# The low halves of the split weights: formed by an accumulating DMA in place of a VectorE subtraction

## The chip, the core and the metric

The kernel runs as one program on one core of a Trainium2 chip. The metric is the device time of one execution in microseconds (us). The engines named below are TensorE (PE in the profile, with its weight loads as PEld), VectorE (DVE), ScalarE (ACT), GpSimd (POOL) and SyncE (SP), beside the 16 DMA engines of the core that move data between HBM and the on-chip memory (SBUF).

## The reference

Two transformer-like blocks work on 512 tokens of 2048 features; the first one adds 16 meta tokens ahead of them. Cut to what matters here:

```python
# first block
proj = einsum('bld,dc->blc', rmsnorm(h, pre_norm_g), w_in)      # q, k, v, gates of two mixers
ya = gqa_axial_mixer(qa, ka, va, ...) * silu(ga)                # softmax attention, 8 heads
yb = diff_attn_mixer(qb, kb, vb, ...) * silu(gb)                # difference of two softmaxes, 8 heads
h = h + rmsnorm(einsum('blc,cd->bld', concat([ya, yb]), w_out), post_norm_g)
# second block
q, k, v, g_sb, x_lru, g_lru = split(einsum('bsd,de->bse', rmsnorm(h, norm_gain_2), w_in_2))
y_sb = stick_breaking_attention(q, k, v) * silu(g_sb)           # 8 heads
y_lru = rg_lru(causal_conv(x_lru), ...) * silu(g_lru)           # 8 blocks
h = h + einsum('bse,ed->bsd', concat([y_sb, y_lru]), w_out_2)
```

All of it is float32. Most of the arithmetic is in the four projections, whose weights are read from HBM.

## The kernel before

**Products in halves.** TensorE multiplies in a format with a shorter mantissa (`F32R`). So each float32 operand is split: the high half is its rounding to that format, the low half what is left of it, and a product is the sum of three: high by high, high by low, low by high (`PASSES`, line 282). The function `split` (line 147) forms the halves with two instructions: line 148 rounds on ScalarE, line 149 subtracts the high half from the float32 value on VectorE. The activations stand split in the tile `big`, from the start of each block on. The weights are split while the kernel runs.

**Weights.** The host packs each weight into units, and each unit into two half units of 128 partitions by 1024 columns (512 KB). `_sequence` lists the 296 half units in the order in which TensorE uses them; some stand there twice, since the last column pairs of the first output projection (O1) and the first projections of the second block (XL) are done for one half of the tokens at a time. `load_next` (line 257) brings the next half unit: SP issues its load into a tile `wraw` (three buffers), and `split` forms the two halves in a tile `wsp` (three buffers): `w[:, 0]` is the high half and `w[:, 1]` the low one. `take` (line 273) is called when TensorE's program comes to a half unit, and loads ahead until two further ones are on their way (`AHEAD = 2`). With three `wsp` buffers, half unit i+2 goes into the buffer of half unit i-1, so its split can begin when TensorE has done its last product with i-1.

**Products per half unit.** A half unit serves 24 products of 512 columns in most places (`fm_real`, and `tm` over four token tiles), and 48 of 264 columns where the meta tokens are in it (`fm_all`). In 64 half units one after the other it serves less: 32 of O1 serve 12 products of 512 columns, for two token tiles, and 32 of XL serve 24 products of 256 columns. This is called the short stage below. In `tm` the last unit of a run takes both of its halves at once and goes through them token tile by token tile: six products with the first half, six with the second, and so on. This is called a pair below. The kernel ends with four single units of the last output projection (O2), which are four pairs, one after the other.

**Order.** TensorE's instructions stand in the order in which the generators are traced: `main_work` yields the projections, and the side generators (scores, softmax, recurrences, norms) are taken in between by due times that count the time of the products traced. Each of the other engines works through its own queue in order; a step there waits on semaphores. ScalarE and VectorE do the side work (exponentials, reductions, gates) beside the splits. GpSimd has little before the change: parts of the rotary embedding (line 450), the bias rows (653), one product per head (725), eight products of the recurrence (833), and the masks of the stick-breaking scores (881), each of which stands between two steps of ScalarE (880 and 884).

The lines that the change and the prediction touch: 148 and 149 (the two passes of the split), 181 (every product and every weight load of TensorE), 266 (the load of a half unit), 1129 to 1147 (the last output projection).

Of the kernel before, what the change touches and what calls it, by code (L numbers as in the profile page):

```python
# [74 lines left out]


def _sequence():
    """The order in which the weight units are used; the last column pairs of the first output projection and
    the first projections of the second block are read twice, for the two halves of the tokens."""
    seq = [("VA", 0), ("VA", 1)] + [("QA0", kg) for kg in range(4)]  # L80
    seq += [("GA", i) for i in range(8)] + [("QA1", kg) for kg in range(4)] + [("GB", i) for i in range(8)]
    for h in range(8):
        seq += [("QB", h), ("KB", h), ("VB", h)]
    seq += [("O1", 0, kg) for kg in range(3)] + [("O1", 1, kg) for kg in range(4)] + [("O1", 0, 3)]
    seq += [("O1", n, kg) for _ in range(2) for n in (2, 3) for kg in range(4)]
    seq += [("XL", b) for _ in range(2) for b in range(8)]
    seq += [("GL", b) for b in range(8)] + [("GS", b) for b in range(8)]
    for c in range(4):
        if c % 2 == 0:
            seq += [("v", c // 2, kg) for kg in range(4)]  # L90
        seq += [("qk", c, kg) for kg in (QK_LAST if c == 3 else range(4))]
    seq += [("O2", n, kg) for n in range(4) for kg in (0, 2, 3)] + [("O2", n, 1) for n in range(4)]
    return [(("KA", i), h) for h in range(2) for i in range(2)] + [(u, h) for u in seq for h in range(2)]
# [3 lines left out]
def hybrid_two_block_kernel(ctx: ExitStack, tc: tile.TileContext, wp, xT, xtok, par, lvec, cst, rg, pg, lruw, out):  # L97
# [22 lines left out]
        return pss_pool[0].tile([P, 2, 512], F32, tag="pss", name="pss")  # L120

    def pst_banks():
        """The two banks as tiles of their own."""
        return pss_pool[0].tile([P, 512], F32, tag="bank", name="bank", bufs=2)

    def ptt():
# [33 lines left out]
            dve.scalar_tensor_tensor(y, t, 1.5, y, op0=ALU.add, op1=ALU.mult)  # L160
        return y

    # ------------------------------------------------- the tensor engine's order
    # The projections and the pieces of everything else are generators; the tensor engine takes their
    # instructions in the order traced here. A step waits for keys: `ready` has the time by which what a
    # key names is there, counted in the time of the products traced so far (`clock`).
    order_only = mybir.DependencyInfo(mybir.DependencyClass.NoSync, mybir.DependencyReason.DATA)
    state = {"clock": 0.0, "last": None}
    ready = {"pss": 0.0, "ptt": 0.0, "pmt": 0.0, "pt": 0.0, "calm": 0.0}
# [79 lines left out]
        o, n = PAR_COLS[name]  # L249
        return prm[:, o : o + n]  # L250

    # ------------------------------------------------- weights
    AHEAD = 2
    seq = _sequence()
    loaded = []

    def load_next(n=1024):
        """The next half unit, in pieces of n columns."""
        if len(loaded) == len(seq):
            return  # L260
        unit, h = seq[len(loaded)]
        raw = T([P, 1024], "wraw", F32, 3)
        w = T([P, 2, 1024], "wsp", F32R, 3)
        loaded.append(w)
        for c in range(0, 1024, n):
            nc.sync.dma_start(raw[:, c : c + n], wp[UIDX[unit], h, :, c : c + n])
            split(w[:, 0, c : c + n], w[:, 1, c : c + n], raw[:, c : c + n])
            if c + n < 1024:
                yield

# [11 lines left out]
    PASSES = ((0, 0), (0, 1), (1, 0))  # L282

    def fm(unit, ps, after_kt=None):
        """Features on partitions; ps: list of (PSUM AP, token columns of big)."""
        for kt in range(KT):
            if kt % 8 == 0:
                w = take(unit, kt // 8)
            for pi, (ws, xs) in enumerate(PASSES):
                lhs = w[:, ws, (kt % 8) * P : (kt % 8 + 1) * P]  # L290
                for ap, (a, b) in ps:
                    mm(ap, lhs, big[:, xs, kt, a:b], kt == 0 and pi == 0, kt == KT - 1 and pi == 2)
                yield
            if after_kt:
                after_kt(kt)

    def fm_two(units, ps, lag):
        """Two units side by side, the second one some steps behind."""
        w = [None, None]
        for i in range(KT + lag):  # L300
            for u, kt in ((0, i), (1, i - lag)):
                if 0 <= kt < KT:
                    if kt % 8 == 0:
                        w[u] = take(units[u], kt // 8)
                    for pi, (ws, xs) in enumerate(PASSES):
                        for c in range(2):
                            mm(ps[u][:, c, :HL], w[u][:, ws, (kt % 8) * P : (kt % 8 + 1) * P],
                               big[:, xs, kt, c * HL : (c + 1) * HL], kt == 0 and pi == 0, kt == KT - 1 and pi == 2)
                        yield
            if i == KT - 1:  # L310
                act.copy(halves(kvraw[0]), ps[0][:, :, :HL])
                post(("kv", 0), 1000)
# [5 lines left out]
        return fm(unit, [(ps[:, 0, :], (x0, x0 + NTOK))])  # L318

    def tm(units, x0, evac, kgs=range(4), toks=range(NT), before_unit=None, after_unit=None, chore=None):  # L320
        """Tokens on partitions; evac(token tiles, their sums) takes the results pair by pair;
        chore: a piece of work for every other step."""
        tiles = {p: pjt() for p in sorted({t // 2 for t in toks})}
        accs = {t: tiles[t // 2][:, t % 2, :] for t in toks}
        for i, unit in enumerate(units):
# [27 lines left out]
                after_unit(kg)  # L353
        post("calm", 2500)

    # ------------------------------------------------- constants, tokens
    act.preload_act_table_set("natural_log_exp_and_others")
    nc.sync.dma_start(prm, par)
    make_identity(nc, ident)
# [49 lines left out]
        dve.tensor_scalar(hg[:, 0:1], par_of("subg"), 0.5 * (1.0 - LAMBDA_INIT), None, op0=ALU.mult)  # L409
        dve.tensor_scalar(hg[:, 1:2], par_of("gq2"), P ** -0.5, None, op0=ALU.mult)  # L410

    # columns of ar in the first block
    kvraw = [ar[:, i * L : (i + 1) * L] for i in range(4)]
    CB = 2560
    cq, sq_ = ar[:, CB : CB + 512], ar[:, CB + 512 : CB + 1024]
# [5 lines left out]
    qs_, ks_, vs_ = ar[:, 4608:5120], ar[:, 5120:5648], ar[:, 2560:3088]  # L421
    osb, osq, orr = ar[:, 3088:3600], ar[:, 3600:4112], ar[:, 1824:2336]

    # ------------------------------------------------- shared pieces
    def diag(r, n=P):
        dg = et(P)
        dve.tensor_scalar(dg[:n, :n], ident[:n, :n], r, None, op0=ALU.mult)
# [14 lines left out]
        split(big[:, 0, s, :NTOK], big[:, 1, s, :NTOK], ybuf[:, s, :])  # L442

    def rope(x, rn, n, c, s, t1, u):
        """x [P, n, 128] (normalised in place), rn [P, n]; the result lands in t1."""
        v4 = lambda a: a.rearrange("p n (h two c) -> p n h two c", h=2, two=2)
        dve.tensor_tensor(x, x, rn.unsqueeze(2).broadcast_to([P, n, P]), ALU.mult)  # L447
        dve.tensor_tensor(blocks(t1), x, blocks(c), ALU.mult)
        for a in range(2):
            pool.tensor_tensor(v4(blocks(u))[:, :, :, a, :], v4(x)[:, :, :, 1 - a, :], v4(blocks(s))[:, :, :, a, :],  # L450
                               ALU.mult)
        dve.tensor_tensor(t1, t1, u, ALU.add)

    def tile_cols(j):
        """Columns of the real tokens' tiles, and of the meta tokens as the last one."""
        return slice(NM + j * P, NM + (j + 1) * P) if j < NT else slice(0, NM)

    def v_tiles(src, tail_i, r=None):
        """src [P d, L]: halves with tokens on partitions, the meta tokens stacked in vtail."""
        vt = T([P, 2, 4, P], "vv", F32R, 2)  # L460
        tp = flat(pst())
        for j in range(5):
            n = P if j < 4 else NM
            tr(tp[:n, j * P : (j + 1) * P], src[:, tile_cols(j)], ident)
        tp3 = blocks(tp[:, :512])
        if r is not None:
            vb, vbt = et(512), et(P)
            dve.tensor_tensor(blocks(vb), tp3, r[:, 0:4].unsqueeze(2).broadcast_to([P, 4, P]), ALU.mult)
            dve.tensor_scalar(vbt[:NM, :], tp[:NM, 512:640], r[:NM, 4:5], None, op0=ALU.mult)
            main_, tail_ = blocks(vb), vbt[:NM, :]  # L470
        else:
            main_, tail_ = tp3, tp[:NM, 512:640]
        split(vt[:, 0], vt[:, 1], main_)
        vs = vtail[tail_i]
        act.copy(vs[0:16, :], tail_)
        act.copy(vs[32:48, :], tail_)
        dve.tensor_tensor(vs[64:80, :], tail_, f(vs[0:16, :]), ALU.subtract)
        return vt, vs

    def pv_steps(h, tag, e, cols, vt, vs, use, extra=()):  # L480
        """Weighted sums over the keys, by halves of the queries; use(half, sums) takes them."""
        for hf in range(2):
            yield when("pt", "ptt", (tag, h, 2 * hf))
            hold("pt")
# [29 lines left out]
            post("pmt", 1300)  # L514
            use(hf, o)

    # ------------------------------------------------- side work, first block
    kt_ = [None]
    va = [None, None]
    lnload = [None, None]  # L520
# [208 lines left out]
        post(("normed", h))  # L729
        post(("y", 8 + h), 5000)  # L730

    # ------------------------------------------------- between the blocks
    yt = blocks(yflat, D)
    pgb = ar[:, 0:2048]

# [40 lines left out]
        if p:  # L776
            room["e"] = 4

    # ------------------------------------------------- RG-LRU
    cw = par_of("cw").rearrange("p (b i) -> p b i", i=4)  # L780
    cb = par_of("cb")

# [55 lines left out]
                dve.scalar_tensor_tensor(y, ybuf[:, i, :], 0.5, y, op0=ALU.mult, op1=ALU.mult)  # L838
                post(("xlused", i))

    # ------------------------------------------------- stick breaking
    raws = [blocks(ar[:, i * 2048 : (i + 1) * 2048], 512) for i in range(3)]
    gains = (hg[:, 1:2], par_of("gk2"))

# [315 lines left out]
    run(main_work(), sides)  # L1160


# [1 line left out]
def _pack(inputs):  # L1164
    import numpy as np

# [74 lines left out]
```

## Time and profile before

| | |
|---|---|
| time, median of 3 runs | 1752.49 us (1752.18 to 1752.86) |
| profiled execution, from first to last instruction | 1751.1 us |
| TensorE granted clock, mean | 1.000 |
| bytes moved by DMA | 185.81 MB, 106 GB/s over the span |
| of these read from HBM | 175.89 MB |
| DMA share of 16 engines, queue of SP's loads | 31.7% |
| loads of half units | 295 of 512 KB and 4 of 128 KB (the first one in four pieces) |

The profile is that of one execution, on the one core that is used; no time beside the span is given for it, and the span is 1.4 us shorter than the median of the runs. A group of instructions is shown by its line, engine, operation and the tiles that it writes and reads, with their count, busy time and mean duration; behind that stands how long the engine stood idle ahead of them and what ended that idle time. A row of the timeline gives start, duration, engine, line, operation and count, and in brackets the idle time ahead of it with its releaser. Products overlap in TensorE's pipeline, so a product's duration is longer than the time from one product to the next.

### The profile page before, as it was taken

To read this page: it belongs to the slowest core of one execution; us is meant where nothing else is said; L and a number is where in the kernel's file an instruction comes from. 1 tells how busy PE (TensorE), PEld (TensorE's weight loads), DVE (VectorE), ACT (ScalarE), POOL (GpSimd) and SP (SyncE) were. 2 spreads that over 40 slices of the span, in tenths; PEclk is the share of its full clock that TensorE was granted. 3 is DMA by queue.
4 is the path that set the end of the run, shared out by engine and by line. 5 is a ranking of instruction groups with operands and counts; after the bars stand their busy time and mean duration, and the time that the engine had idled before them with its cause. 6 is when DMAs were issued, how large, how long until landed. Compare 5 with 4: busy or idle time off the path is not lost.

```text
span 1751.1 us, 23788 instructions
## 1 busy us (share of the span) xinstructions
PE 1739.6 (99%) x9496; PEld 1484.8 (85%) x9496; DVE 1023.0 (58%) x1694; ACT 785.5 (45%) x1276; POOL 89.6 (5%) x83
## 2 busy tenths in 40 slices
PE   8999999999999999999999999999999999999998
PEld 8888888889998888988788998888888888888887
DVE  5748635863566666785458858843323564575433
ACT  6334423443445454564345537832222654564311
POOL 0101001100001100100000001100000000010000
PEclk9999999999999999999999999999999999999999
DMA  9321222212221222212367653222222222432223
GB/s 312 117 97 60 73 73 87 82 61 85 73 73 61 67 67 73 71 63 73 120 216 269 213 196 122 91 97 96 97 95 90 80 72 85 137 117 84 85 91 126
DMA packets 53854, 185.81 MB, mean 106 GB/s; under 512 B 6112, under 2 KB 7776, under 8 KB 52064
## 3 DMA queue, kind: packets, MB, share of 16 engines
q1 hardware_dynamic: 53744, 184.30, 31.7%
q8 instruction: 74, 1.21, 0.3%
q14 instruction: 36, 0.29, 0.1%
HBM read 175.89 MB, written 8.39 MB: 105 GB/s over the span
## 4 chain that ended last, share of the span: by engine, by line
PE 94%; DVE 2%; DMA 1%; issue 1%; ACT 0%; POOL 0%; SPq 0%; DVEq 0%; ACTq 0%; POOLq 0%
PE pj L181 81%; PE pss L181 4%; PE pmt L181 4%; PE ptt L184 2%; PE pmt L184 1%; PE bank L181 1%; PE pss L184 1%; DVE wsp L149 0%; DMA ybuf<-in_xtok 0%; DMA wraw<-in_wp 0%; DMA e<-in_xT 0%; ACT wsp L148 0%; POOL ar L450 0%; POOL ybuf L450 0%; DVE big L376 0%
## 5 line engine op out<-in xcount | busy, mean ns | idle before, releaser
L181 PE MATMUL pj<-big,wsp 128*128 128x264 f32 (+2 forms) x4608 | 814.9, 333 | 6.2 <-ACT big L375 5.4
L181 PEld LDWEIGHTS pj<-big,wsp 128*128 128x128 f32 x4608 | 687.8, 189 | 94.9 <-ACT big L375 5.4
L181 PE MATMUL pj<-wsp,big 128*128 128x512 f32 x3072 | 737.5, 397 | 0.6 <-DVE big L149 0.6
L181 PEld LDWEIGHTS pj<-wsp,big 128*128 128x128 f32 x3072 | 569.8, 188 | 132.3 <-DVE big L149 0.9
L149 DVE TENSOR_TENSOR wsp<-wraw,wsp 128x1024 fp32r<-128x1024 f32 (+1 forms) x299 | 363.3, 1215 | 389.1 <-ACT wsp L148 388.7
L148 ACT CAST wsp<-wraw 128x1024 fp32r<-128x1024 f32 (+1 forms) x299 | 310.8, 1040 | 504.9 <-PE pj L181 400.3
L683 ACT ACTIVATE e<-e,sm 128x528 f32<-128x528 f32 x64 | 47.2, 737 | 91.9 <-DVE sm L680 91.5
L148 ACT CAST pt<-ptt 128x512 fp32r<-128x512 f32 (+2 forms) x96 | 50.4, 525 | 77.5 <-PE ptt L184 77.3
L181 PE MATMUL pss<-kk,qq 128*128 128x264 f32 x448 | 83.6, 301 | 0.0
L149 DVE TENSOR_TENSOR pt<-ptt,pt 128x512 fp32r<-128x512 f32 (+2 forms) x96 | 59.5, 619 | 35.9 <-ACT pt L148 35.1
L181 PEld LDWEIGHTS pss<-kk,qq 128*128 128x128 f32 x448 | 66.8, 188 | 12.8 <-issue 0.2
L181 PEld LDWEIGHTS pmt<-pt,vv 128*128 128x128 f32 x528 | 69.1, 190 | 3.6
L680 DVE CUSTOM_DVE_ANT_0 e<-pss,ar 128x528 f32<-128x528 f32 x64 | 45.1, 704 | 45.8 <-PE pss L181 45.5
L181 PE MATMUL pmt<-pt,vv 128*128 128x256 f32 (+1 forms) x528 | 69.6, 280 | 0.0
L184 PE MATMUL ptt<-ident,e 128*128 128x128 f32 x336 | 52.6, 273 | 0.1
L184 PEld LDWEIGHTS ptt<-ident,e 128*128 128x128 f32 x336 | 40.6, 140 | 7.0 <-DVE e L626 0.5
L432 DVE TENSOR_TENSOR e<-pj,rbc 128x512 f32<-128x512 f32 x32 | 22.0, 688 | 39.8 <-PE pj L181 39.8
L881 POOL TENSOR_SCALAR_AFFINE_SELECT e<-e 128x128 f32<-128x128 f32 x32 | 15.7, 490 | 476.2 <-ACT e L880 474.2
L653 POOL TENSOR_SCALAR ar<-ar 128x912 f32<-128x912 f32 x8 | 22.5, 2816 | 262.5 <-DVE sm L680 257.9
L623 ACT ACTIVATE e<-pss,sm 128x528 f32<-128x528 f32 x32 | 22.4, 701 | 23.5 <-DVE sm L621 23.4
L450 POOL TENSOR_TENSOR ar<-ar 128x256 f32<-128x256 f32 x16 | 18.4, 1172 | 242.9 <-DVE ar L447 242.9
L890 ACT ACTIVATE e<-e 128x128 f32<-128x128 f32 (+3 forms) x32 | 15.0, 470 | 28.8 <-DVE e L889 28.5
(200 smaller groups left out, 1175.5 us busy)
## 6 DMA issues: line engine op xcount, KB each, us to landing
wraw<-in_wp SPq DMA_DIRECT2D x295, 512.0 KB, 3.5
e<-in_xT SPq DMA_DIRECT2D x16, 264.0 KB, 4.6
ybuf<-in_xtok SPq DMA_DIRECT2D x4, 1024.0 KB, 6.8
ar<-in_xtok SPq DMA_DIRECT2D x4, 1024.0 KB, 5.6
h1d<-ybuf SPq DMA_DIRECT2D x4, 1024.0 KB, 5.3
ybuf<-h1d SPq DMA_DIRECT2D x12, 256.0 KB, 3.5
out<-ybuf SPq DMA_DIRECT2D x12, 256.0 KB, 2.2
ar<-in_pg SPq DMA_DIRECT2D x1, 1024.0 KB, 4.8
```

Source lines behind the costliest of these rows:

```text
L148: act.copy(hi, src)
L149: dve.tensor_tensor(lo, src, f(hi), ALU.subtract)
L181: _queue(nc.tensor.matmul(out, lhsT, rhs, start=start, stop=stop).ins, cost)
L184: _queue(nc.tensor.transpose(out, in_, identity).ins, 110.0)
L432: dve.tensor_tensor(g, g_ps, rb, ALU.mult)
L450: pool.tensor_tensor(v4(blocks(u))[:, :, :, a, :], v4(x)[:, :, :, 1 - a, :], v4(blocks(s))[:, :, :, a, :], ALU.mult)
L623: act.activation(halves(x), sv, AF.Exp, bias=nm, accum_out=l[:, 0:1])
L653: pool.tensor_scalar(bias, dist, 2.0 ** (-(h + 1)), None, op0=ALU.mult)
L680: dve.tensor_tensor_reduce(out=halves(x), in0=s[:, :, :HL], in1=halves(bias[:, b0 : b0 + L]), scale=1.0, scalar=3e38, op0=ALU.add, op1=ALU ...
L683: act.activation(x, x, AF.Exp, scale=-1.0, bias=nm, accum_out=l[:, m : m + 1])
L881: pool.affine_select(z[:, t * P : w], z[:, t * P : w], [[-1, P]], ALU.is_gt, -1e30, base=0, channel_multiplier=1)
L890: act.activation(c, c, AF.Exp)
```

## The change

From the thirteenth half unit on, the low half is formed otherwise. ScalarE makes two passes over `wraw`: the high half as before, and the negated value, rounded alike, into the place of the low half. Then GpSimd issues a DMA that reads the same half unit from HBM once more and adds it onto what stands there: the weight minus its high half. VectorE's subtraction is gone for these 284 half units; the first twelve are split as before. Half units are now read from HBM twice. The remaining lines of the diff take comments away, and the seven new lines shift the line numbers behind them by seven.

```diff
@@ load_next
-            nc.sync.dma_start(raw[:, c : c + n], wp[UIDX[unit], h, :, c : c + n])
-            split(w[:, 0, c : c + n], w[:, 1, c : c + n], raw[:, c : c + n])
+            src = wp[UIDX[unit], h, :, c : c + n]
+            nc.sync.dma_start(raw[:, c : c + n], src)
+            if late:
+                act.copy(w[:, 0, c : c + n], raw[:, c : c + n])
+                act.mul(w[:, 1, c : c + n], raw[:, c : c + n], -1.0)
+                pool.dma_start(w[:, 1, c : c + n], src, accum_op=ALU.add)
+            else:
+                split(w[:, 0, c : c + n], w[:, 1, c : c + n], raw[:, c : c + n])
```

with `late = len(loaded) > 12` ahead of the loop, counted with the present half unit.

Three places in the instruction streams. First TensorE in one of the last four pairs. `pj` is the tile that gathers the sums, the two `wsp` tiles are the pair's halves (the numbers are those of the tiles), and in brackets stand the semaphores of the engines that a product waits for; DMASW is that of GpSimd's DMAs. Before the change:

```order
L181 MATMUL pj_14541<-wsp_14476,big_69 128x512 [waits DVE_49,Activation_49]
L181 MATMUL pj_14541<-wsp_14476,big_69 128x512 x5
L181 MATMUL pj_14541<-wsp_14481,big_69 128x512 [waits Activation_49]
L181 MATMUL pj_14541<-wsp_14481,big_69 128x512
L181 MATMUL pj_14541<-wsp_14481,big_69 128x512 [waits DVE_49]
L181 MATMUL pj_14541<-wsp_14481,big_69 128x512 x3
```

And with the change:

```order
L181 MATMUL pj_14823<-wsp_14756,big_69 128x512 [waits DVE_49,Activation_49]
L181 MATMUL pj_14823<-wsp_14756,big_69 128x512
L181 MATMUL pj_14823<-wsp_14756,big_69 128x512 [waits DMASW0_49]
L181 MATMUL pj_14823<-wsp_14756,big_69 128x512 x3
L181 MATMUL pj_14823<-wsp_14762,big_69 128x512 [waits Activation_49]
L181 MATMUL pj_14823<-wsp_14762,big_69 128x512
L181 MATMUL pj_14823<-wsp_14762,big_69 128x512 [waits DMASW1_49]
L181 MATMUL pj_14823<-wsp_14762,big_69 128x512 x3
```

The products stand in the same order; the third product of each half, the first that reads the low half, now waits for GpSimd's DMA, where it waited for VectorE.

Second ScalarE, at the last steps of the stick-breaking heads, ahead of the last pairs (`e` are scores, `pt` their transposes, `big` the activations). Before:

```order
L148 CAST wsp<-wraw 128x1024
L886 ACTIVATE e<-e 128x512
L890 ACTIVATE e<-e 128x512
L148 CAST wsp<-wraw 128x1024
L148 CAST pt<-ptt 128x3x128
```

With the change, where line 270 is the pass for the high half, 271 the negated one, and 893 and 897 are the old 886 and 890:

```order
L270 CAST wsp<-wraw 128x1024
L893 ACTIVATE e<-e 128x512
L271 ACTIVATE wsp<-wraw 128x1024
L897 ACTIVATE e<-e 128x512
L270 CAST wsp<-wraw 128x1024
L271 ACTIVATE wsp<-wraw 128x1024
L148 CAST pt<-ptt 128x3x128
```

Each half unit has a second pass of the same size here, now and then with a step of the side work between the two.

Third GpSimd, from the recurrence to the stick-breaking masks. Before:

```order
L653 TENSOR_SCALAR ar<-ar 128x912
L725 TENSOR_TENSOR ar<-ar 128x512 x2
L833 TENSOR_TENSOR ar<-ar 128x512 x8
L881 AFFINE_SELECT e<-e 128x128 x32
L1237 UNCONDITIONAL_BRANCH
```

With the change, where 840 and 888 are the old 833 and 881:

```order
L840 TENSOR_TENSOR ar<-ar 128x512
L272 DMA wsp<-in_wp 128x1024 x41
L888 AFFINE_SELECT e<-e 128x128 x2
L272 DMA wsp<-in_wp 128x1024
L888 AFFINE_SELECT e<-e 128x128
```

The accumulating DMAs stand in GpSimd's queue between its other steps; each of them waits for ScalarE's second pass over its half unit, and the steps behind it wait with it.

More of the change, by code (lines that the diff above doesn't have):

```diff
@@ L264, in load_next @@
         loaded.append(w)
+        late = len(loaded) > 12
         for c in range(0, 1024, n):
-            nc.sync.dma_start(raw[:, c : c + n], wp[UIDX[unit], h, :, c : c + n])
-            split(w[:, 0, c : c + n], w[:, 1, c : c + n], raw[:, c : c + n])
+            src = wp[UIDX[unit], h, :, c : c + n]
[6 more added lines that the diff above has]
+                split(w[:, 0, c : c + n], w[:, 1, c : c + n], raw[:, c : c + n])
             if c + n < 1024:
```

## The prediction

> **What bounds the kernel now.** I read the page's busy table first, then its slices, then what TensorE (PE) waited for, then stretches of the span. In the busy table the span stands first; of the two slice rows, DMA is the busy share of the 16 engines in tenths.
>
> ```profile
> span 1751.1 us, 23788 instructions
> PE 1739.6 (99%) x9496; PEld 1484.8 (85%) x9496; DVE 1023.0 (58%) x1694; ACT 785.5 (45%) x1276; POOL 89.6 (5%) x83
> ...
> DMA  9321222212221222212367653222222222432223
> ```
>
> PE is without work for 1751.1 - 1739.6 = 11.5 us, and VectorE (DVE) is busy for little more than half. Where the 11.5 us lie, the stretches tell (us, then busy us with instruction counts, granted clock, DMA share, GB/s):
>
> ```profile
> core 0: us, PE busy (x) PEld busy (x) DVE busy (x) ACT busy (x) POOL busy (x), PEclk, DMA share, GB/s
> 0.00:100.00 100.00, 93.66 (x582) 83.53 (x583) 57.54 (x123) 48.27 (x67) 7.01 (x11) 1.00 0.58 198
> ...
> 872.00:1064.00 192.00, 192.00 (x1241) 173.86 (x1240) 134.24 (x186) 98.12 (x115) 0.00 (x0) 1.00 0.65 219
> 1064.00:1150.00 86.00, 86.00 (x373) 69.60 (x372) 73.23 (x92) 68.45 (x90) 12.44 (x8) 1.00 0.30 99
> ...
> 1700.00:1751.00 51.00, 46.65 (x201) 37.30 (x199) 19.54 (x25) 7.37 (x7) 0.00 (x0) 0.99 0.35 124
> ```
>
> The first 100 us hold 6.3 us of them, the last 51 us 4.4 us, all the rest 0.8 us. PE is the bound, at full clock, and it almost never waits for a weight:
>
> ```profile
> PE pj L181 <- ACT big L375: 5.4, 1, 5.4
> ...
> PE pj L181 <- DVE wsp L149: 0.4, 1, 0.4
> ```
>
> So nothing that DVE does can be bought back on PE, except 0.8 us. What matters is how soon a half unit of weights becomes usable after its buffer falls free. Call that the **turnaround**, and the time between the buffer's release and PE's need the **allowance**. The two passes that now follow the release:
>
> ```profile
> L149 DVE TENSOR_TENSOR wsp<-wraw,wsp 128x1024 fp32r<-128x1024 f32 (+1 forms) x299 | 363.3, 1215 | 389.1 <-ACT wsp L148 388.7
> L148 ACT CAST wsp<-wraw 128x1024 fp32r<-128x1024 f32 (+1 forms) x299 | 310.8, 1040 | 504.9 <-PE pj L181 400.3
> ```
>
> In this and the next group the numbers are busy us and mean ns of one, then idle time ahead and its releaser. ScalarE (ACT) mostly stands idle until PE releases the buffer (400.3 us), then takes 1.05 us, then DVE 1.22 us: a turnaround of 2.3 us.
>
> ```profile
> L181 PE MATMUL pj<-wsp,big 128*128 128x512 f32 x3072 | 737.5, 397 | 0.6 <-DVE big L149 0.6
> ```
>
> **The allowances.** A product is on record for 0.40 us, and the next one starts before it ends. The timeline of the last four pairs (the output projection's single units, both halves taken at once):
>
> ```profile
> 1657.04 89.61 PE L181 MATMUL pj<-wsp,big 128*128 128x512 f32 x384
> ...
> 1700.59 1.05 ACT L148 CAST wsp<-wraw 128x1024 fp32r<-128x1024 f32 x1 [8.73 <-PE pj L181]
> 1701.67 1.23 DVE L149 TENSOR_TENSOR wsp<-wraw,wsp 128x1024 fp32r<-128x1024 f32 x1 [3.98 <-ACT wsp L148]
> ...
> 1711.76 1.05 ACT L148 CAST wsp<-wraw 128x1024 fp32r<-128x1024 f32 x1 [8.72 <-PE pj L181]
> ...
> 1722.94 1.05 ACT L148 CAST wsp<-wraw 128x1024 fp32r<-128x1024 f32 x1 [8.72 <-PE pj L181]
> ...
> 1734.11 1.05 ACT L148 CAST wsp<-wraw 128x1024 fp32r<-128x1024 f32 x1 [8.72 <-PE pj L181]
> ```
>
> 89.61/384 = 0.233 us per product. The buffer of a pair's first half falls free 6 products before the pair's end. The next pair needs the refilled buffer's low half after 6 products of its own first half and 2 with the new high half (the wait stands on the third product): 14 x 0.233 = 3.3 us, less the 0.16 us (0.40 - 0.233) by which the release trails the next product's start: 3.1 us. Today 2.3 us fit.
>
> In the short stage (872 to 1064 us) a half unit serves two token tiles or 256 columns:
>
> ```profile
> 1010.91 45.07 PE L181 MATMUL pj<-big,wsp 128*128 128x256 f32 x377
> ...
> 1019.99 1.05 ACT L148 CAST wsp<-wraw 128x1024 fp32r<-128x1024 f32 x1 [1.80 <-PE pj L181]
> ...
> 1022.84 1.05 ACT L148 CAST wsp<-wraw 128x1024 fp32r<-128x1024 f32 x1 [1.80 <-PE pj L181]
> ```
>
> A half unit lasts 2.85 us there. With three buffers and two halves of lead the allowance is two half units: 5.7 - 0.16 + 0.24 (two products of 0.12 us) = 5.8 us. 64 half units go through this stage. Elsewhere halves last 24 x 0.233 = 5.6 us, which allows 11.2 - 0.16 + 0.47 = 11.5 us, or more where other products lie between; only the second half after a pair taken at once has less, as here:
>
> ```profile
> 1295.65 1.05 ACT L148 CAST wsp<-wraw 128x1024 fp32r<-128x1024 f32 x1 [2.86 <-PE pj L181]
> 1295.69 14.59 PE L181 MATMUL pj<-wsp,big 128*128 128x512 f32 x62
> ```
>
> 6 products to the pair's end, 24 of the next half and 2: 32 x 0.233 - 0.16 = 7.3 us. Counting such places by the order of the units and the casts' starts, eleven have no other work to lengthen them.
>
> **What the change costs, step by step.** 284 of the 296 half units lose the 1.22 us subtraction: 345 us off DVE, worth at most the 0.8 us above. ACT gets 284 second passes at the cast's 1.05 us, 298 us in all, and GpSimd (POOL) 284 DMAs that read the half unit again and add it. The turnaround becomes 1.05 + 1.05 + 0.1 (three hand-overs of about 0.04 us, the gap from cast to subtraction above) + the accumulating transfer. The trace shows no such transfer. The nearest rows (KB each, median us to landing):
>
> ```profile
> wraw<-in_wp SPq DMA_DIRECT2D x295, 512.0 KB, 3.5
> ybuf<-in_xtok SPq DMA_DIRECT2D x4, 1024.0 KB, 6.8
> ar<-in_xtok SPq DMA_DIRECT2D x4, 1024.0 KB, 5.6
> h1d<-ybuf SPq DMA_DIRECT2D x4, 1024.0 KB, 5.3
> ...
> prm<-in_par SPq DMA_DIRECT2D x1, 49.5 KB, 1.8
> ...
> DMA to landing us min/median/max: 2.3/3.5/8.1
> ```
>
> From below: a plain load of this size, 3.5 us. From above: the longest weight load of this run, 8.1 us. An add must read both addends, 1024 KB for 512 KB written, so I take a 1024 KB load's 5.6 us: turnaround 7.8 us. For the engines' time: 219 GB/s at a share of 0.65 is 337 GB/s when all are busy, so 512 KB occupy them 1.56 us, and an add that reads twice 3.1 us.
>
> The Trainium skill (Collectives: The Full Stack, section "The bandwidth ceiling: the fold count and why AG ≠ RS ≠ AR") says that a reducing transfer needs two source reads and gives a ratio of 1.93 to a copy. No run here shows it yet; by it the short stage is the dearer of its two readings below, by a plain copy's cost the cheap rival.
>
> The sum, against the span of 1751.1 us:
> - Last four pairs: 4 x (7.8 - 3.1) = 19 us. A like pair ahead of the short stage: 5 us.
> - Eleven second halves: 11 x (7.8 - 7.3) = 6 us.
> - Short stage, by turnaround: two half units go through per turnaround, so 64 x (7.8 - 5.8)/2 = 64 us. By engine time: 0.65 x 192 = 125 us of transfers are there, 64 x 3.1 = 198 come on top, 323 - 192 = 131 us. The lines are not exclusive: loads and adds share the engines and lengthen each other. I take 110, nearer to the second, since the share is 0.65 before anything is added.
> - Side work: between 1064 and 1150 us ACT is busy for 68.45 of 86 us and gets 14 more passes, 15 us: 97%. In-order ACT then delays casts and recurrences; bounds 0 to 20, taken as 8. The masks' selects on POOL stand behind adds that wait for ACT; their chain runs ahead of PE, and I take 0 (bounds 0 to 15; the cover gone, it is POOL's time per issue at 32 places).
> - DVE: between 0 and -0.8 us, taken as 0.
>
> 19 + 5 + 6 + 110 + 8 = 148 us. A span of 1899 us, and with the 1.4 us by which the runs' median of 1752.5 exceeds this span, **1900 us**, 8% slower.
>
> **The rivals.**
> - *Cheap add*: it costs as a plain load, 3.5 us and 1.56 us of engine time. Turnaround 5.7: last pairs 10, the like pair 3, second halves 0, short stage 125 + 100 - 192 = 33 us, side work 2: 48 us, 1800 us. For it: the weight load's own row. Against it: both addends must be read, and POOL issues it. The Trainium skill (DMA: Bandwidth & Descriptors, "Anatomy of one DMA — SWDGE (gpsimd) path") gives 2.0 us plus bytes/436e3, an estimate of 3.2 us for a plain copy of 512 KB issued by POOL; no run here shows it, and by it this rival's 48 us would be a little less.
> - *Dear add*: three times a plain load's engine time, 4.7 us, and 8.1 us to landing, so a turnaround of 10.3. Last pairs 29, like pair 7, second halves 33, short stage 125 + 301 - 192 = 234, side work 10: 313 us, 2065 us. For it: POOL issues each transfer in its own order, with waits, and the short stage's slow loads (8.1 us at most). Beyond 11.5 us every half unit would pay.
> - *Not slower*: DVE's late subtractions were what held PE, and the add is ready in time everywhere. It decides only if the add lands within 3.1 - 2.2 = 0.9 us of ACT's second pass in the last four pairs; the shortest landing quoted is 1.8 us, for 49.5 KB. The gain ends at the 0.8 us of idle PE: 1752 us.
>
> That PE would not wait for the adds at all is excluded: the changed order has 284 such waits, on the third product of each half.
>
> **How the numbers follow.** Forecast (1840 to 1960) 0.45; cheap (1775 to 1840) 0.23; dear (above 1960) 0.29; not slower 0.03. Range 1785 to 2070: it takes in the cheap and the dear sums and leaves out about 0.15, mostly an add dearer than three loads. A difference of 0.2%, 3.5 us, is about what a measurement of this kernel tells from none. Chances: faster 0.01, same 0.02, slower 0.97.
>
> **What would show it.** The adds' time to landing (5.6 forecast) and the DMA share of the short stage (near 1, with that stage about 300 us long). PE idle for some 5 us before each of the last four pairs, waiting for a DMA into wsp. Idle PE of about 150 us, most of it in the short stage. ACT busy for about 1085 us, DVE for about 680. It is wrong if the short stage keeps its 192 us, if PE's new waits name ACT or POOL rather than the add, or if halves with an allowance of 11.5 us are late, which would mean an add of over 9 us.

## The result, and the profile after

| | before | with the change |
|---|---|---|
| median, 4 runs each (range) | 1752.67 us (1752.18 to 1753.20) | 2018.81 us (2009.34 to 2022.04) |
| ratio (95% interval) | | 1.1507 (1.1492 to 1.1521) |
| profiled execution: time, span | span 1751.1 us | 2022.04 us, span 2020.1 us |
| granted clock, mean | 1.000 | 0.957 |

The change makes the kernel 15% slower. On the page of the changed kernel I first read the busy table, the rows of slices and the queues:

```profile
span 2020.1 us, 24254 instructions
PE 1823.0 (90%) x9496; PEld 1534.4 (76%) x9496; DVE 699.4 (35%) x1410; ACT 1046.0 (52%) x1560; POOL 320.8 (16%) x367
...
PE   8999999999999999977677768999988999999966
...
PEclk9999999999999999988888988999999999999988
DMA  8565576566666556669999996768867666865653
...
q0 software_dynamic: 40896, 148.92, 40.9%
q1 hardware_dynamic: 53744, 184.30, 29.1%
...
wraw<-in_wp SPq DMA_DIRECT2D x295, 512.0 KB, 4.7
wsp<-in_wp POOLq DMA_DIRECT2D x284, 512.0 KB, 7.9
```

The span grew by 269.0 us, and it grew in two ways. PE's idle time went from 11.5 to 2020.1 - 1823.0 = 197.1 us, 185.6 more. PE's busy time went from 1739.6 to 1823.0 us, 83.4 more, for the same 9496 products. So they took longer, and the clock row says why for the most part: (1 - 0.957) x 2020.1 = 87 us of full clock were not granted. By the clock records of this trace PE was busy for 141 us at a clock of 0.50, which cost it 70 us; the other 17 fell into its idle time and cost nothing. The last 13 us are for the most part no slower work: the last product ahead of each of the 73 waits counts with its whole duration, 0.16 us more than the time to a next one, an estimated 12 us. The added idle time has one cause, as PE's waits show (total, times, longest):

```profile
PE pj L181 <- DMA wsp<-in_wp: 186.0, 73, 8.3
```

Where the time went, the same eight stretches show in both traces. They are cut at the starts of ScalarE's casts of the same half units (118, 122, 186, 202, 218, 266 and 290, counted from zero). Columns: us, busy us of PE, PEld, DVE, ACT, POOL with counts, clock, DMA share, GB/s. Before:

```profile
0.00:851.00 851.00, 844.56 (x5058) 737.33 (x5059) 526.98 (x990) 381.87 (x678) 61.46 (x43) 1.00 0.26 88
851.00:874.00 23.00, 22.42 (x96) 17.72 (x95) 10.35 (x15) 8.88 (x17) 0.00 (x0) 1.00 0.46 147
874.00:1065.00 191.00, 191.00 (x1236) 173.04 (x1235) 135.16 (x188) 98.07 (x116) 0.18 (x1) 1.00 0.65 218
1065.00:1163.00 98.00, 98.00 (x424) 79.29 (x423) 76.66 (x95) 70.10 (x91) 12.25 (x8) 1.00 0.30 101
1163.00:1252.00 89.00, 89.00 (x385) 72.01 (x384) 30.64 (x33) 21.07 (x24) 0.00 (x0) 1.00 0.29 95
1252.00:1552.00 300.00, 300.00 (x1399) 245.90 (x1398) 146.13 (x230) 138.68 (x239) 9.30 (x20) 1.00 0.30 97
1552.00:1702.00 150.00, 150.00 (x717) 123.82 (x716) 77.88 (x123) 60.55 (x110) 6.38 (x12) 1.00 0.26 84
1702.00:1751.00 49.00, 44.65 (x192) 35.67 (x190) 19.21 (x25) 6.31 (x6) 0.00 (x0) 0.99 0.36 129
```

And with the change:

```profile
0.00:865.00 865.00, 849.11 (x5056) 739.93 (x5057) 405.05 (x884) 477.41 (x783) 145.55 (x149) 1.00 0.64 150
865.00:901.00 36.00, 26.44 (x100) 20.58 (x99) 7.78 (x12) 12.27 (x21) 2.61 (x3) 0.86 0.60 157
901.00:1225.00 324.00, 234.04 (x1230) 200.46 (x1229) 62.45 (x126) 156.50 (x180) 55.98 (x65) 0.86 0.92 230
1225.00:1342.00 117.00, 104.21 (x428) 83.45 (x429) 56.00 (x77) 86.87 (x109) 24.28 (x25) 0.94 0.69 160
1342.00:1431.00 89.00, 89.00 (x383) 71.83 (x382) 11.25 (x17) 35.86 (x40) 13.77 (x16) 1.00 0.88 188
1431.00:1763.00 332.00, 310.88 (x1406) 251.21 (x1405) 93.03 (x183) 182.83 (x287) 48.23 (x68) 0.97 0.71 165
1763.00:1935.00 172.00, 155.72 (x712) 125.63 (x712) 52.64 (x99) 82.30 (x132) 24.30 (x35) 0.97 0.65 144
1935.00:2020.00 85.00, 53.62 (x191) 41.29 (x189) 11.21 (x18) 11.97 (x13) 6.03 (x7) 0.84 0.46 118
```

Row by row the stretches grew by 14, 13, 133, 19, 0, 32, 22 and 36 us, 269 in all. The third row is the short stage, with half of the loss: 90 us of idle PE, and 43 us more of busy PE for nearly as many products, at a clock of 0.86. The fifth row holds 16 adds, as the fourth does, and loses nothing. The last row is the four last pairs: 31.4 us idle, where it was 4.4.

The timeline around the second of these pairs shows what one add does (start, duration, engine; in brackets the idle time ahead; the last row is cut off where the view ends):

```profile
1944.69 12.77 PE L181 MATMUL pj<-wsp,big 128*128 128x512 f32 x48 [8.26 <-DMA wsp<-in_wp]
1954.28 1.05 ACT L270 CAST wsp<-wraw 128x1024 fp32r<-128x1024 f32 x1 [17.12 <-issue]
1955.24 1.05 ACT L271 ACTIVATE wsp<-wraw 128x1024 fp32r<-128x1024 f32 x1
...
1956.32 0.34 SPq L268 DMA_DIRECT2D wraw<-in_wp  x1
1956.59 0.86 POOL L272 DMA_DIRECT2D wsp<-in_wp  x1 [18.27 <-ACT wsp L271]
...
1964.40 2.08 PE L181 MATMUL pj<-wsp,big 128*128 128x512 f32 x4 [6.94 <-DMA wsp<-in_wp]
```

ScalarE's second pass ends at 1956.29. That releases two things: the add, and 0.27 us ahead of it SP's next load, since the pass was also the last reader of the `wraw` buffer. PE goes on at 1964.40, 7.8 us after the issue of the add. And it goes on slowly, as the clock of the next two stretches shows (same columns as above):

```profile
1964.40:1967.80 3.40, 3.40 (x8) 2.75 (x9) 0.00 (x0) 0.00 (x0) 0.00 (x0) 0.50 0.84 190
1967.80:1977.50 9.70, 9.70 (x41) 7.49 (x40) 2.58 (x4) 3.14 (x4) 0.84 (x1) 0.98 0.17 64
```

For 3.4 us behind the gap 8 products run at a clock of 0.50, and then 41 in 9.7 us at 0.98.

### The profile page after: what moved, and what is told of

Its sections match the earlier page's. It is cut to its first block, busy times and chain, and to the rows that moved or that the text cites. A ratio compares the mean times of both kernels' runs of the same rounds, so it can differ in the third digit from the quotient of the medians.

```text
span 2020.1 us, 24254 instructions
## 1 busy us (share of the span) xinstructions
PE 1823.0 (90%) x9496; PEld 1534.4 (76%) x9496; DVE 699.4 (35%) x1410; ACT 1046.0 (52%) x1560; POOL 320.8 (16%) x367
## 4 chain that ended last, share of the span: by engine, by line
PE 61%; DMA 22%; issue 14%; ACT 2%; POOL 0%; DVE 0%; SPq 0%; POOLq 0%; DVEq 0%; ACTq 0%
PE pj L181 51%; DMA wsp<-in_wp 21%; PE pss L181 4%; PE pmt L181 3%; PE ptt L184 2%; PE pmt L184 1%; PE pss L184 1%; DMA ybuf<-in_xtok 0%; PE bank L181 0%; ACT wsp L271 0%; ACT wsp L270 0%; DMA wraw<-in_wp 0%; DMA e<-in_xT 0%; ACT big L382 0%; ACT L838 0%
## 5 line engine op out<-in xcount | busy, mean ns | idle before, releaser
L181 PE MATMUL pj<-wsp,big 128*128 128x512 f32 x3072 | 789.0, 414 | 128.6 <-DMA wsp<-in_wp 128.6
L181 PE MATMUL pj<-big,wsp 128*128 128x264 f32 (+2 forms) x4608 | 845.5, 341 | 63.6 <-DMA wsp<-in_wp 57.3
L181 PEld LDWEIGHTS pj<-big,wsp 128*128 128x128 f32 x4608 | 710.6, 196 | 160.3 <-DMA wsp<-in_wp 63.7
L181 PEld LDWEIGHTS pj<-wsp,big 128*128 128x128 f32 x3072 | 595.4, 198 | 286.4 <-DMA wsp<-in_wp 149.3
L270 ACT CAST wsp<-wraw 128x1024 fp32r<-128x1024 f32 x284 | 297.2, 1046 | 573.9 <-issue 295.3
L272 POOL DMA_DIRECT2D wsp<-in_wp x284 | 246.0, 866 | 1454.8 <-ACT wsp L271 1341.1
L271 ACT ACTIVATE wsp<-wraw 128x1024 fp32r<-128x1024 f32 x284 | 299.1, 1053 | 0.1
L1008 DVE TENSOR_TENSOR ybuf<-pj,ar 128x512 f32<-128x512 f32 x12 | 8.3, 690 | 121.8 <-PE pj L181 115.9
L1109 DVE TENSOR_REDUCE sm<-e 128x4 f32<-128x512 f32 x16 | 9.9, 679 | 76.0 <-ACT e L1108 76.0
L604 DVE TENSOR_REDUCE sm<-ar 128x4 f32<-128x512 f32 x8 | 5.4, 679 | 73.5 <-ACT ar L602 73.5
```

The lines of the kernel that those rows point to most:

```text
L181: _queue(nc.tensor.matmul(out, lhsT, rhs, start=start, stop=stop).ins, cost)
L270: act.copy(w[:, 0, c : c + n], raw[:, c : c + n])
L271: act.mul(w[:, 1, c : c + n], raw[:, c : c + n], -1.0)
L272: pool.dma_start(w[:, 1, c : c + n], src, accum_op=ALU.add)
L1109: dve.tensor_reduce(ss[:, 4 * t : 4 * t + 4], blocks(sq), axis=AX.X, op=ALU.add)
```

## The experiments

Each kernel is the changed one with the edit shown. Ratios are to the kernel before, on the same chip.

**1. The change without its add.** This leaves the low halves at the negated high half.

```diff
-                pool.dma_start(w[:, 1, c : c + n], src, accum_op=ALU.add)
```

> Leaves out the accumulating DMAs, so the low half stays the negated weight; both ACT passes stay. Theory A (the loss is the turnaround, 10.2 us where 2.3 were, of which the add's landing is 7.7, plus the lower clock that follows PE's waits): the turnaround is 2.3 us again, nothing is late, 1753 us within 4, clock 1.00. Rival B (ACT's 284 second passes cost side work their time): 1765 us or more, PE waiting for ACT or for side work.

Measured: 1752.50 us, ratio 0.9998 (0.9988 to 1.0007). Its busy table:

```profile
span 1750.1 us, 23537 instructions
...
PE 1738.6 (99%) x9496; PEld 1484.0 (85%) x9496; DVE 694.3 (40%) x1410; ACT 1041.0 (59%) x1558; POOL 77.4 (4%) x83
```

ScalarE has its 284 more passes, VectorE is rid of 329 us, and the time is that of before. The passes and VectorE's relief together change nothing, and the whole loss hangs on the add.

**2. A plain copy in place of the add,** from the same queue at the same places. The low half is then the whole weight.

```diff
-                pool.dma_start(w[:, 1, c : c + n], src, accum_op=ALU.add)
+                pool.dma_start(w[:, 1, c : c + n], src)
```

> The DMA from GpSimd overwrites instead of adding, so the low half is the whole weight; bytes read and written otherwise alike. Theory A1 (the landing of 7.7 us is mostly GpSimd's path, the second read adds one packet time for each of 8 rows per engine, 8 x 0.165 = 1.3 us): packets of 160 ns, landing about 6.4 us, time about 1940 us. Rival A2 (the add itself is what is slow): landing 3.5 to 4.7 us as for the plain loads of SP, about 1800 us. Rival A3 (all of it is GpSimd's path): landing 7.7, about 2010 us.

Measured: 1849.07 us, ratio 1.0546 (1.0525 to 1.0567). From its page, the queue of GpSimd's copies and the two transfers (KB, median us to landing):

```profile
q0 software_dynamic: 40896, 148.92, 22.4%
...
wraw<-in_wp SPq DMA_DIRECT2D x295, 512.0 KB, 3.6
wsp<-in_wp POOLq DMA_DIRECT2D x284, 512.0 KB, 4.6
```

And of its stretches the short stage:

```profile
879.00:1130.00 251.00, 210.47 (x1227) 180.56 (x1227) 61.41 (x122) 155.45 (x178) 33.89 (x64) 0.95 0.86 296
```

A copy occupies the 16 engines for 0.224 x 1847.1 / 284 = 1.46 us, the change's add for 0.409 x 2020.1 / 284 = 2.91 us: twice as long. The packet records say the same: the median packet of 4 KB takes 159 ns in SP's loads of the changed kernel, 328 ns in its adds, and 174 ns in these copies. To landing, GpSimd's copy takes 1.0 us more than SP's load, and the add 3.3 us more than the copy: the landing is that of the second theory, while the time lies between the first two. Of the 266 us of the change, the plain copy alone makes 96 (1849.07 - 1752.92); the adding makes the rest. The short stage, at 251 us, is already 60 us over its 191, with a share of 0.86.

**3. Adds without the loads beside them:** 62 half units of the short stage take their passes from an older half unit, so the two parts still sum to the weight but are not its high and low half; their loads are gone, while the adds stay.

```diff
-        raw = T([P, 1024], "wraw", F32, 3)
+        i = len(loaded)
+        bare = 122 <= i < 184
+        raw = held[0] if bare else T([P, 1024], "wraw", F32, 3)
+        held[0] = raw
...
-            nc.sync.dma_start(raw[:, c : c + n], src)
+            if not bare:
+                nc.sync.dma_start(raw[:, c : c + n], src)
```

> 62 half units of the short stage get no load by SP: ACT's passes read an older half unit, the adds stay. It takes 62 x 1.56 = 97 us of the engines' time out of that stage and leaves the turnaround as it is, but for less company on the engines. Theory E (that stage, 324 us long at a DMA share of 0.9, is bound by the engines' time): it falls to about 230 us, total about 1925 us. Theory A (it is bound by the turnaround of one half unit): 64 x 10.2/2 less the overlap, about 300 us, landing 7.7, total about 1995 us.

Measured: 1971.16 us, ratio 1.1243 (1.1220 to 1.1265), between the two expectations. The stretch of the short stage:

```profile
904.00:1174.00 270.00, 218.07 (x1229) 187.28 (x1229) 61.15 (x122) 156.17 (x179) 56.09 (x65) 0.92 0.80 156
```

And the adds' landing in it, from 910 to 1170 us:

```profile
DMA to landing us min/median/max: 5.2/5.5/10.6
```

With no loads beside it, an add lands in 5.5 us; in the same window of the changed kernel the median is 8.1. The stage falls from 324 to 270 us, not to its old 191. At a share of 0.80 the engines are no longer full, so what is left I put down to the turnaround and to the clock, at 0.92, by which PE is busy for 218 us instead of 191; no run separates the two.

**4. Adds only where the allowance is 11.5 us or more:** 188 of the 284. The short stage with the pair ahead of it, and 31 further half units, second halves most of them, are split by VectorE.

```diff
+    TIGHT = (15, 17, 39, 41, 109, 111, 117, 185, 223, 225, 231, 233, 239, 241, 247, 249, 255,
+             257, 263, 265, 269, 271, 275, 277, 281, 283, 287, 289, 291, 293, 295)
...
-        late = len(loaded) > 12
+        i = len(loaded) - 1
+        late = i >= 12 and not 119 <= i < 184 and i not in TIGHT
```

> Adds only where the allowance is 11.5 us or more and PE's run before is not taken as a pair: the split by VectorE stays for the short stage, the second halves behind pairs and the last four pairs; about 190 adds remain. Theory A: turnaround 10.2 us, less than 11.5 everywhere, nothing late, clock 1.00, 1753 to 1762 us. Rival B (engine load, ACT's passes or GpSimd's queue cost by themselves): two thirds of the loss outside the short stage stays, over 1800 us.

Measured: 1778.40 us, ratio 1.0155 (1.0132 to 1.0177), outside what either theory said. PE's waits for adds are down from 73 to 7:

```profile
PE pj L181 <- DMA wsp<-in_wp: 15.1, 7, 4.8
```

Most of the loss lies in the stretch behind the short stage (half units 186 to 202, where the gates and the recurrence keep ScalarE busy): it took 118 us, where the fourth row of the table of before has 98.

```profile
1063.00:1181.00 118.00, 105.19 (x426) 83.58 (x425) 57.69 (x80) 86.95 (x109) 24.17 (x24) 0.94 0.68 156
```

There ScalarE starts its passes some 2 us after the buffer's release in the median (0.04 to 6.8 us). The longest wait, 4.8 us, has another form of the same cause: four steps of side work stand between the two passes (lines 272 and 273 here).

```profile
1152.18 1.05 ACT L272 CAST wsp<-wraw 128x1024 fp32r<-128x1024 f32 x1
...
1157.02 1.04 ACT L273 ACTIVATE wsp<-wraw 128x1024 fp32r<-128x1024 f32 x1
```

The adds behind the seven waits land in 6.5 to 8.6 us, no more than elsewhere. An allowance counts only what ScalarE leaves of it.

**5. The load behind the add:** GpSimd issues both, so the next load cannot start ahead of the add.

```diff
-            nc.sync.dma_start(raw[:, c : c + n], src)
+            (pool if late else nc.sync).dma_start(raw[:, c : c + n], src)
```

> The loads of the half units from the thirteenth on are issued by GpSimd, behind the add that the same ACT pass releases, in place of SP; the arithmetic is that of the change. Theory C (of the add's landing of 7.7 us about 2.3 are lost to the SP load that starts 0.27 us ahead of it on the same DMA engines; an add with the engines to itself lands in 5.3 us, as in the run without these loads): landing 5.3 to 5.8, turnaround about 8, total about 1880 us. Rival (the add is that slow whoever else loads): landing 7.5 or more, total about 2010 us.

Measured: 1922.56 us, ratio 1.0965 (1.0944 to 1.0987). The adds' landing over the run, from its page:

```profile
wsp<-in_wp POOLq DMA_DIRECT2D x284, 512.0 KB, 5.6
```

And the stretch of the short stage:

```profile
885.00:1187.00 302.00, 224.27 (x1232) 189.08 (x1230) 61.59 (x123) 156.56 (x180) 92.02 (x129) 0.91 0.96 246
```

The add lands in 5.6 us instead of 7.9, with the same bytes on the same engines. So the 2.3 us were the load that was issued just ahead of it. The time fell by 96 us, not by as much as I expected: in the short stage the engines are busy for 0.96 of 302 us, and the order of issue saves only 22 of 324 us there. The edit also has a price in that stage. The loads now come later, and ScalarE waits for them (us, times, longest):

```profile
ACT wsp L270 <- DMA wraw<-in_wp: 26.1, 7, 9.1
```

In the changed kernel it waits so for 1.6 us in this stage. How much of the 302 us is due to that stays open.

**6. PE kept busy in the short stage:** the first product of each of its half units is repeated, which adds products to the sums.

```diff
+                if pi == 1 and kt % 8 == 0 and unit[0] == "XL":
+                    for _ in range(12):
+                        mm(ap, w[:, 0, :P], big[:, 0, kt, a:b], False, False)
...
+                        if pi == 1 and k2 == 0 and t == min(toks) and len(toks) == 2:
+                            for _ in range(6):
+                                mm(accs[t], big[:, 0, kt, x0 + t * P : x0 + (t + 1) * P], w[:, 0, :512], False, False)
```

> The first product of each half unit of the short stage is repeated behind its second product, 6 times at 512 and 12 times at 256 columns (1.4 us at full clock), so PE works while it waits for the add; the output then lacks the reference's sums. Theory D (PE's clock falls to half in the gaps, and the products that free the next buffer then take longer, which adds to the loop of turnaround and products): the clock in that stage rises from 0.86 to 0.97 or more, the stage falls from 324 to about 295 us although PE has 90 us more work, total about 1990 us. Rival (the turnaround alone sets the stage; the lower clock only fills the gaps): stage 324 us or more, total 2019 us or more.

Measured: 1964.76 us, ratio 1.1206 (1.1163 to 1.1250). The short stage:

```profile
889.00:1206.00 317.00, 296.96 (x1830) 261.69 (x1829) 69.44 (x136) 166.01 (x191) 57.63 (x67) 0.98 0.95 240
```

The clock is back at 0.98 and PE works for 297 of 317 us, yet the stage is only 7 us shorter, between the two expectations. The engines are busy for 0.95 x 317 = 301 us here and for 0.92 x 324 = 298 us in the changed kernel. So this stage is set mostly by the transfers, and the slow clock mostly filled gaps that PE had anyway. The rest of the run was 47 us faster too, so the time is below both expectations; the repeats also move side work in TensorE's order behind the stage, so that part is confounded and stays open.

**7. Adds only at the four places of the last pairs** that need them soonest; everything else is split as before.

```diff
-        late = len(loaded) > 12
+        late = len(loaded) - 1 in (289, 291, 293, 295)
```

> Adds for four half units only, the second halves of the last four pairs; all others are split by VectorE. Theory A with the landing of 7.7 us as in the changed kernel: 4 x (10.2 - 3.1) = 28 us and a little for the clock, 1781 to 1788 us. Rival C (with less company on the engines the add lands in 5.3 to 6 us): 4 x (8.2 - 3.1) = 20 us, about 1773 us.

Measured: 1787.89 us, ratio 1.0200 (1.0183 to 1.0217): 35 us for four adds. The timeline of the last pairs:

```profile
1711.57 13.66 PE L181 MATMUL pj<-wsp,big 128*128 128x512 f32 x48 [7.77 <-DMA wsp<-in_wp]
1732.12 13.64 PE L181 MATMUL pj<-wsp,big 128*128 128x512 f32 x48 [6.89 <-DMA wsp<-in_wp]
1751.09 12.77 PE L181 MATMUL pj<-wsp,big 128*128 128x512 f32 x48 [5.33 <-DMA wsp<-in_wp]
1769.62 11.82 PE L181 MATMUL pj<-wsp,big 128*128 128x512 f32 x40 [5.76 <-DMA wsp<-in_wp]
```

The waits sum to 25.8 us, and the time is what the first theory said. PE's busy time on the page is 1747.7 us, 8 more than before: 48 products take 13.7 us behind a gap of 7 us, where 48 x 0.233 = 11.2 us is full speed.

**8 and 9. The adds where they fit, twice narrowed.** Experiment 4 with VectorE splitting the 16 half units behind the short stage too (173 adds left), and then also every half unit whose allowance, less ScalarE's lateness in the profile of the kernel before, is under 11.2 us (162 left; the list has 41 entries then).

```diff
-        late = i >= 12 and not 119 <= i < 184 and i not in TIGHT
+        late = i >= 12 and not 119 <= i < 200 and i not in TIGHT
```

> As the run with adds only at wide allowances, but VectorE's split also for the 16 half units of the GL projection, where ACT is busy and starts the passes 2 us late; about 175 adds remain. Theory A (its 7 waits of 15 us, and the clock behind them, came from that stretch): 1753 to 1758 us. Rival (engine load or GpSimd's queue cost by themselves): 1770 us or more as before.

> As the second run with adds at wide allowances, but also without the half units whose first ACT pass starts late in the profile of the kernel before, so that allowance less that delay stays under 11.2 us; 162 adds remain. Theory A (an add costs nothing where turnaround and ACT's delay fit): no wait for an add, 1753 us within 3. Rival (a rest is the price of the adds' presence): 1757 us or more.

Measured: 1759.88 us, ratio 1.0037 (1.0024 to 1.0050), a little beyond what was expected, with five waits left; then 1753.34 us, ratio 1.0004 (0.9995 to 1.0014). Of the second, PE's one wait for an add:

```profile
PE pj L181 <- DMA wsp<-in_wp: 0.9, 1, 0.9
```

And the adds' landing:

```profile
wsp<-in_wp POOLq DMA_DIRECT2D x162, 512.0 KB, 7.7
```

162 adds that land in 7.7 us cost nothing, because nobody waits. They bring nothing either: PE was the bound, and VectorE had time.

**10. PE kept busy behind the last waits:** experiment 7 with the first product of each such second half repeated 24 times.

```diff
+                        if len(units) == 1 and unit[0] == "O2" and pi == 1 and k2 == 0 and t == 0 and h == 1:
+                            for _ in range(24):
+                                mm(accs[t], big[:, 0, kt, x0 + t * P : x0 + (t + 1) * P], w[:, 0, :512], False, False)
```

> Adds for the second halves of the last four pairs as in the run with four adds, and the first product of each such half repeated 24 times ahead of the wait (5.6 us at full clock); the output then lacks the reference's sums. Theory D (of its 35 us about 26 are waits and 8 to 9 the half clock behind them): the clock stays at 1.00, the products of each pair take 11.2 us again, total 1778 to 1781 us with 22 us more work on PE. Rival (the longer pairs have another cause, or the filler delays): 1788 us or more.

Measured: 1780.62 us, ratio 1.0160 (1.0145 to 1.0176). Its busy table:

```profile
PE 1762.6 (99%) x9592; PEld 1502.0 (84%) x9592; DVE 1019.0 (57%) x1690; ACT 788.6 (44%) x1280; POOL 93.5 (5%) x87
```

And the timeline behind its first two waits (the second row runs on through the next pair, which no longer waits):

```profile
1711.56 17.03 PE L181 MATMUL pj<-wsp,big 128*128 128x512 f32 x72 [2.71 <-DMA wsp<-in_wp]
1729.87 33.89 PE L181 MATMUL pj<-wsp,big 128*128 128x512 f32 x144 [1.28 <-DMA wsp<-in_wp]
```

96 more products, 96 x 0.233 = 22 us of work, and the kernel is 7 us faster than without them. They stand in the gaps: the waits sum to 4.2 us instead of 25.8, the mean clock is 1.000 instead of 0.992, and the real products behind no longer crawl.

## Why the prediction was right, and where it was not

The direction and the main mechanism were right: the add takes the place of a 1.2 us subtraction in the turnaround, nothing bought on VectorE counts, and the short stage loses most. But the forecast put three quarters of the loss there (110 of 148 us), and it has half (133 of 269). The sum was 121 us short. The time is inside the range because the range took in the dear add, not because the sum was near: it lies above the 1840 to 1960 us that stood for the forecast, in the part that had a chance of 0.29.

- **DVE at nothing, ACT's passes at 8 us.** Both are shown by experiment 1, together 0. DVE came to 699 us (forecast about 680), ACT to 1046 (about 1085).
- **Landing, 5.6 us.** It measured 7.9 in the median. The failed step is that I took "a 1024 KB load's 5.6 us" for the add as it stands in this kernel. The size was right for an add alone (5.5 us in experiment 3, 5.6 in 5), with some luck, since the rows of 1024 KB to choose from went from 5.3 to 6.8 us. What I left out is that ScalarE's second pass also releases SP's next load, which goes first. The turnaround is 10.3 us and not 7.8, the median over the 284 adds from the first pass's start to the landing. Its parts, by their medians, are 0.95 to the start of the second pass, 1.05 for that pass, 0.3 to GpSimd's issue, and 7.9 to landing.
- **Engine time, 3.1 us per add.** It measured 2.91, twice a plain copy's 1.46. The Trainium skill (Collectives: The Full Stack, "The bandwidth ceiling: the fold count and why AG ≠ RS ≠ AR") says of a ReduceScatter over four ranks that its add needs two source reads, and has 1.93 as the measured ratio to an AllGather, which copies. The trace agrees with the ratio: the packets give 328/159 = 2.06 against SP's loads and 328/174 = 1.89 against GpSimd's copies. That a second read is what doubles it, no run here shows.
- **Short stage, 110 us.** It measured 133. Of my two readings the engine time, 131, came nearest, and experiments 3, 5 and 6 point to it as the main limit: without its loads the stage fell by 54 us, while a sooner landing and a restored clock each left it over 300 us long. That 131 so nearly meets 133 is partly luck. The sum had 323 us of transfers that leave no gap; measured are 298 us, and the engines are not full for the other 26. The reading by turnaround was set up wrongly: with PE waiting, three half units pass per turnaround and one half unit's products, not two per turnaround. At the measured 10.3 us that makes an estimated 64 x ((10.3 + 2.85)/3 - 2.85) = 98 us, so it is not far behind, and no run tells how the two add up.
- **Last pairs, 19 us; the like pair, 5 us.** They measured 36 and 13. With 10.3 us in place of 7.8 the first of these terms would have been 4 x (10.3 - 3.1) = 29 us; 31.4 - 4.4 = 27 us of idle time were seen (25.8 in experiment 7). The other 53.6 - 44.7 = 9 us are the slow clock behind the waits, a term that the sum did not have.
- **Second halves, 6 us, and elsewhere, nothing.** This is the largest miss: outside the pairs and the short stage 14 + 19 + 32 + 22 = 87 us were lost, where these terms and the side work had 14. A turnaround of 10.3 us misses 7.3 us by 3 us and not by 0.5. And where ScalarE is late with a pass, even 11.5 us do not suffice, as experiments 4, 8 and 9 show place by place. "Bounds 0 to 20, taken as 8" priced ScalarE's delay as its own work, when its price is that it comes on top of a turnaround already near the allowance.
- **The clock.** No term had it. A wait of several us on PE was priced at its own length, but behind it products run at 0.50 for 3.4 us at a time. The Trainium skill (TensorE: Matmul & The Clock Gate, "Part 1: The HAM clock gate (the "warmup" mystery)") says that the clock is gated to half after an idle window and freed by work, in windows of 3413 ns. The trace agrees: in the clock records of the changed kernel 36 of the 37 slow pieces last 3.4 or 6.8 us, at 0.50. They sum to 177 us, and PE is busy in 141 of these, which cost it 70. This is worth what experiment 10 shows where PE is the limit, and little where the transfers are (experiment 6).
- **The rivals.** The *cheap add*'s 1800 us fell with both its prices: even the plain copy of experiment 2 lands in 4.6 us, not 3.5, and makes 1849 us. By the formula of the Trainium skill (DMA: Bandwidth & Descriptors, "Anatomy of one DMA — SWDGE (gpsimd) path") it would have been an estimated 3.2 us; the runs do not bear that out as a time from issue to landing. The *dear add*, at 2065 us, was nearest, by errors that cancel: its landing (8.1) and turnaround (10.3) are about those measured (7.9 and 10.3), while its 4.7 us of engine time is 1.6 times too much. So its short stage is 101 us too dear, which covers the 57 us that its other terms lack (79 against 136). *Not slower* is excluded.
- **The signs named.** DMA share near 1 in a short stage of about 300 us: 0.92 in 324. Some 5 us idle before each last pair: 5.7 to 8.3. Idle PE of about 150 us, most of it in the short stage: 197, with 90 there. Halves with 11.5 us late "would mean an add of over 9 us": in experiment 4 they are late in places with adds of 6.5 to 8.6 us, because ScalarE is late.

## What to carry to other kernels

Price work that moves from an engine to a DMA by its whole turnaround, from the release of the buffer to the landing, and ask which other transfers the same event releases; set that against the allowance place by place, after taking off how late the issuing engine comes. Where the bound engine waits for some us, add what its clock loses behind the wait, and where engines' time is the limit, count an add as two copies. Work taken from an engine that nobody waits for gains nothing, however much of it there is.

## What the runs showed of the hardware

- An accumulating transfer of 512 KB from HBM into SBUF, issued by GpSimd, lands in 5.5 us, in the median, with no load issued just ahead of it (experiment 3), and in 7.7 to 7.9 us with a load of the same size issued 0.27 us before it. A plain copy by GpSimd, with such a load, lands in 4.6 us and SP's load in 3.5 to 3.6 (4.7 beside the adds).
- GpSimd itself is busy for 866 ns in the mean with an add's issue (246.0 us for 284) and for 539 ns with a copy's (153.1 us).
- Repeating products that nobody needs made a kernel 7 us faster (experiments 7 and 10), since they hold the clock up over a wait (1.000 instead of 0.992).
